# Decoder trunk mixer: where the output weights' low parts stand, and how the conv norm's row sums are formed

## Chip, cores, metric

The kernel runs on one core of a Trainium2 chip. The metric is device microseconds of one execution; the time before is the median of three runs, 1797.14 us (1795.66 to 1797.37). The engines are named as in the profile: PE (TensorE matrix products), PEld (its weight loads), DVE (VectorE), ACT (ScalarE), POOL (GpSimd), SP (SyncE, which issues most transfers). Each engine works through its own queue in order.

## The reference

Two layers, each with a gated feed-forward block, a mixer, and a second feed-forward block, over 512 tokens of width 1024, batch 1, all in float32. The change is in the mixer:

```python
h = rms_norm(x, mix_norm[l])
a, g, q, k, v = jnp.split(h @ w_in[l], splits, axis=-1)

conv_out = conv_module(a, g, conv_w[l], conv_b[l], conv_norm[l])
...
diff_out = diff_attention(q, k, v, rel_bias, lam, lam_init, subln_norm[l])
x = x + jnp.concatenate([conv_out, diff_out], axis=-1) @ w_out[l]

def conv_module(a, g, conv_w, conv_b, conv_norm):
    u = a * jax.nn.sigmoid(g)
    y = lax.conv_general_dilated(u, rhs, ...)   # causal, depthwise, 31 taps, 512 channels
    y = y + conv_b
    return jax.nn.silu(rms_norm(y, conv_norm))  # the norm runs over the 512 channels of a token

# differential attention: 4 heads, two softmax maps each (64 wide), values 128 wide
a = p[:, :, 0] - lam * p[:, :, 1]
o = einsum(a, v);  o = rms_norm(o, subln_g) * (1.0 - lam_init)
```

## The kernel before

**Tiling.** Activations lie with channels on the 128 partitions and the 512 tokens along the row, in 8 blocks of 128 channels. Weights arrive as float32 chunks of 128 x 1024. Each is split into a rounded high part (`whi`, ACT, line 97) and the rest, the low part (`wlo`, line 98, on DVE or POOL as the call says). A product of two float32 matrices is then three products in the faster rounded type (`mm3`: lines 160, 163, 164).

**Order.** The program is written as one stream and a scheduler that is part of the build (`TileContext` with its timeline) puts each engine's instructions into an order of its own choosing, which is then fixed; `keep_in_program_order` holds a single instruction back from being moved ahead of what was written before it. A tile in a pool with n buffers can be written again only when the reader of n tiles earlier is done. PSUM has eight banks, by tag: `sc` 2, `po` 2, `mm` 2, `tp` 1, `y` 1.

**The mixer** (`mixer`). First the projections: conv inputs (`conv_in`), keys and queries (`project`, `to_features`), values (`project_values`). Then two things run side by side.

- The conv branch. `conv_taps(c, n)` forms channel block c of 4. For c = 0 POOL adds all 31 taps (each product on ACT at line 662, each addition on POOL at line 663, into `yp`); for c = 1 and 2 DVE does all taps in a PSUM bank `y` (line 675); for c = 3 POOL does 10 taps and DVE 21, and line 679 joins the two into `u`. `conv_square` squares a block on ACT (line 649) and POOL adds the squares into `csum` (line 650). `conv_finish` then takes the token sums of `csum` over partitions: `rows_rstd` transposes four 128 x 128 blocks into PSUM (line 216), DVE sums each row (line 220) and scales it (line 221), POOL raises it to the power -1/2 (`rs_y`, line 209). `spread` puts the 512 factors on a diagonal (`diag`, DVE, line 236), multiplies by ones so that every partition has them (line 240, bank `y`), and ACT copies that to `rb` (line 244). Then for each of the four blocks: multiply by `rb` (POOL, line 689), tanh (ACT, line 691), the swish's product (DVE, line 692), the high part (ACT, line 693) and the low part (DVE, line 694), which are the right-hand operands of the first half of the output projection.
- Attention. 16 steps (i, h), query block i from 3 down to 0, head h. `softmaxes` makes two score products (line 709; map 0 in an `sc` bank, map 1 in a `po` bank), adds the bias and takes a minimum on DVE (line 713), exponentials and their sums on ACT (line 717), then the small factors on DVE (reciprocal, line 720; `c2`, line 722) and the combined map `e0` (line 723). Line 723 reads the `po` bank, so the score two steps later waits for it. Two steps later `keys_first` transposes the map (line 730) and ACT copies it (line 732); a step after that `values` multiplies by the values (line 739, bank `mm`). After the last head of a block come the block's norm (DVE 746 and 750, POOL 751 and 209, DVE 754 `ov`), and `block_out` transposes it (line 766) and writes its high and low part (ACT 768, DVE 769). The `mm` banks are two, so block 1's value products need block 3's outputs written.

**The output projection** follows (`chunk(wout[...], G)`, line 815): half 0 of the weights times the conv branch, half 1 times attention's outputs. Its low parts are made on POOL. Its first four chunks are loaded long before they are used, and the scheduler may put their low parts wherever POOL seems free. The results go to banks `sc` and `po`, and DVE adds them to x (line 820).

Of the kernel before, what the change touches and what calls it, by code (L numbers as in the profile page):

```python
# [11 lines left out]
F32 = mybir.dt.float32  # L12
# [3 lines left out]
ALU = mybir.AluOpType  # L16
AX = mybir.AxisListType

P = 128
# [4 lines left out]
NT = SEQ // P  # L24
# [3 lines left out]
CC = 512  # L28
CT = CC // P
# [7 lines left out]
EPS = 1e-6  # L37
# [30 lines left out]
def trunk(ctx: ExitStack, tc: tile.TileContext, xt, par, lamv, relb, onehot,  # L68
          gu1, dn1, wag, wqkv, wout, gu2, dn2, out):
    nc = tc.nc  # L70
    V, S, G, T = nc.vector, nc.scalar, nc.gpsimd, nc.tensor

    const = ctx.enter_context(tc.tile_pool(name="const", bufs=1))
    small = ctx.enter_context(tc.tile_pool(name="small", bufs=2))
# [6 lines left out]
    def f32(ap):  # L81
        return ap.bitcast(F32)
# [3 lines left out]
    def bank(tag, name):  # L86
        return psum.tile([P, 512], F32, tag=tag, name=name, bufs=BANKS[tag])
# [4 lines left out]
    def ring(tag, n=1024):  # L92
        dt = F32 if "raw" in tag else F32R
        return wp.tile([P, n], dt, tag=tag, name=tag, bufs=RING[tag])

    def parts_of(raw, hi, lo, eng=None):
        S.activation(hi, raw, AF.Copy)  # L97
        (eng or V).tensor_tensor(out=lo, in0=raw, in1=f32(hi), op=ALU.subtract)  # L98

    def chunk(src, eng=None):  # L100
        raw, hi, lo = ring("wraw"), ring("whi"), ring("wlo")
        nc.sync.dma_start(raw, src)
        parts_of(raw, hi, lo, eng)
        return hi, lo

    def gather(src, blocks, eng=None):
# [51 lines left out]
    def mm3(ps, w, x, start, stop, pin=False):  # L158
        (wh, wl), (xh, xl) = w, x
        first = T.matmul(ps, wh, xh, start=start, stop=False)  # L160
        if pin:
            tc.keep_in_program_order(first)
        T.matmul(ps, wh, xl, start=False, stop=False)  # L163
        T.matmul(ps, wl, xh, start=False, stop=stop)  # L164
# [21 lines left out]
    for k0, k1 in ((0, 1), (1, 4), (4, KT)):  # L186
        h = slice(k0 * P, k1 * P)
# [9 lines left out]
    ones = const.tile([P, P], F32, tag="ones", name="ones")  # L197
# [9 lines left out]
    def rsqrt(v, n, use=""):  # L207
        y = small.tile([P, n], F32, tag=f"rs_y{n}{use}", name="rs_y")
        G.tensor_tensor(y, v, mhalf[:, :n], op=ALU.pow)
        return y  # L210

    def rows_rstd(s, dim, use="", pin=False):

        ps = bank("y", "ps_rows")
        for j in range(NT):
            mm = T.transpose(ps[:, j * P : (j + 1) * P], s[:, j * P : (j + 1) * P], ident)
            if pin:
                tc.keep_in_program_order(mm)
        v = small.tile([P, NT], F32, tag=f"rowv{use}", name="rowv")
        V.tensor_reduce(v, ps.rearrange("p (j c) -> p j c", j=NT), axis=AX.X, op=ALU.add)  # L220
        V.tensor_scalar(v, v, 1.0 / dim, EPS, op0=ALU.mult, op1=ALU.add)
        return rsqrt(v, NT, use), v

    def spread(rc, tag, pin=False, split=False):

        parts, dt, left = [rc], F32, ones
        if split:
            hi = small.tile([P, NT], F32R, tag="rc_hi", name="rc_hi")
            V.tensor_scalar(hi, rc, 1.0, None, op0=ALU.mult)
            lo = small.tile([P, NT], F32, tag="rc_lo", name="rc_lo")  # L230
            V.tensor_tensor(lo, rc, f32(hi), op=ALU.subtract)
            parts, dt, left = [f32(hi), lo], F32R, ones_r
        ps = bank("y", "ps_spread")
        for n, part in enumerate(parts):
            dg = tmp.tile([P, NT, P], dt, tag=("diag", "sq")[n], name="diag", bufs=1 + n)
            V.tensor_tensor(
                dg, ident.unsqueeze(1).broadcast_to([P, NT, P]),
                part.unsqueeze(2).broadcast_to([P, NT, P]), op=ALU.mult,
            )
            mm = T.matmul(ps, left, dg.rearrange("p j c -> p (j c)"), start=n == 0, stop=n == len(parts) - 1)  # L240
            if pin:
                tc.keep_in_program_order(mm)
        r = act.tile([P, SEQ], F32, tag=tag, name=tag)
        S.activation(r, ps, AF.Copy)
        return r
# [254 lines left out]
    nlam, gq, gsub, ghalf = [], [], [], []  # L500
# [35 lines left out]
    def mixer(l, pr, after):  # L536
        with tc.tile_pool(name="mix", bufs=1) as mp, tc.tile_pool(name="mt", bufs=2) as mt:
# [102 lines left out]

            ys = [None] * CT
            csum = mp.tile([P, SEQ], F32, tag="csum", name="csum")

            def conv_square(c, y):
                if c == 0:
                    S.activation(csum, y, AF.Square)
                else:
                    sq = mt.tile([P, SEQ], F32, tag="csq", name="csq", bufs=1)
                    S.activation(sq, y, AF.Square)
                    G.tensor_tensor(csum, csum, sq, op=ALU.add)  # L650

            def conv_taps(c, n):

# [27 lines left out]
                    S.activation(ys[c], y, AF.Copy)  # L681
                conv_square(c, ys[c])

            def conv_finish():
                rcv = spread(rows_rstd(csum, CC, "c")[0], "rb")
                for c in range(CT):
                    z = ys[c]
                    hg = ghalf[l][:, c : c + 1]
                    G.tensor_tensor(z, z, rcv, op=ALU.mult)
                    th = mt.tile([P, SEQ], F32, tag="gl", name="th", bufs=1)  # L690
                    S.activation(th, z, AF.Tanh, scale=hg)
                    V.scalar_tensor_tensor(z, th, 1.0, z, op0=ALU.add, op1=ALU.mult)
                    S.activation(ch[:, c, :], z, AF.Copy, scale=hg)
                    V.scalar_tensor_tensor(cl[:, c, :], z, hg, f32(ch[:, c, :]), op0=ALU.mult, op1=ALU.subtract)
# [5 lines left out]
            def softmaxes(i, h):  # L700
                W = (i + 1) * P
                tq = slice(i * P, W)
                if h == 0:
                    sums[i] = small.tile([P, 2, HEADS], F32, tag="sums", name="sums")
                scs = [bank(tag, "ps_sc")[:, :W] for tag in ("sc", "po")]
                e0 = mt.tile([P, SEQ], F32, tag="e0", name="e", bufs=4)[:, :W]
                sm = sums[i]
                for m in range(2):
                    T.matmul(scs[m], qz[:, m, h, tq], kt[:, h, :W], start=True, stop=True)  # L709

                for m, (sc, e) in enumerate(zip(scs, (e0, scs[1]))):
                    mn = small.tile([P, 1], F32, tag=f"mn{m}", name="mn")
                    V.tensor_tensor_reduce(
                        out=e, in0=sc, in1=row["bias"][:, h, SEQ - W :], scale=1.0, scalar=3e38,
                        op0=ALU.add, op1=ALU.min, accum_out=mn,
                    )
                    S.activation(e, e, AF.Exp, bias=mn, scale=-1.0, accum_out=sm[:, m, h : h + 1])

                r2 = small.tile([P, 1], F32, tag="r2", name="r2")
                V.reciprocal(r2, sm[:, 1, h : h + 1])  # L720
                c2 = small.tile([P, 1], F32, tag="c2", name="c2")
                V.tensor_scalar(c2, r2, nlam[l], sm[:, 0, h : h + 1], op0=ALU.mult, op1=ALU.mult)
                V.scalar_tensor_tensor(e0, scs[1], c2, e0, op0=ALU.mult, op1=ALU.add)
                maps[i, h] = e0

# [47 lines left out]
            def attend(n):  # L773
                if n < len(steps):
                    softmaxes(*steps[n])
                if 2 <= n < len(steps) + 2:
                    keys_first(*steps[n - 2])
                if 3 <= n < len(steps) + 3:
                    values(*steps[n - 3])
                if n >= 5 and steps[n - 5][1] == HEADS - 1:  # L780
                    block_out(steps[n - 5][0])
# [19 lines left out]
                project_values(NT - 2 - 2 * n)  # L801
            for c in range(CT):
                conv_taps(c, POOL_TAPS[c])
            for n in range(2, len(steps) + 5):
                attend(n)
            conv_finish()

            for half, t in ((0, slice(0, SEQ)), (1, slice(SEQ // 2, SEQ)), (1, slice(0, SEQ // 2))):  # L810
                if t.stop == SEQ:
                    w = [None] * 4
                for m in range(KT):
                    if w[m // 2] is None:
                        w[m // 2] = chunk(wout[l, half, m // 2], G)
                    ps = bank(("sc", "po")[m % 2], "ps_out")[:, : t.stop - t.start]
                    for kk in range(4):
                        k = half * 4 + kk
                        mm3(ps, wpart(w[m // 2], (m % 2) * 4 + kk), (ch[:, k, t], cl[:, k, t]), kk == 0, kk == 3)
                    V.tensor_tensor(x[:, m, t], ps, x[:, m, t], op=ALU.add)  # L820

                    if half == 1 and t.start == 0 and m < KT // 2:
                        after(m)
# [103 lines left out]
```

## Time and profile before

| quantity | value |
|---|---|
| median of three runs | 1797.14 us |
| profiled execution, its own time | 1795.63 us |
| its span, first to last instruction | 1793.9 us |
| PE busy | 1783.0 us (99%) |
| DVE, ACT, POOL busy | 1207.6, 897.1, 666.8 us |
| granted TensorE clock | 1.000 over the span |

The span is what the trace covers; the execution's own time has 1.7 us more around it. PE is busy nearly all the time by the page, but a matmul's end is modelled, and matmuls overlap; whether TensorE is held up is read from the starts in its timeline and from its waits.

The main rows that the change touches, with their mean durations:

| row | what | count | mean ns |
|---|---|---|---|
| L98 POOL, 128x1024 | low part of a weight chunk | in the mixer | 2400 |
| L663 POOL | one conv tap's addition | 78 | 1295 |
| L650 POOL | squares into `csum` | 6 | 1292 |
| L216 PE, from `csum` | one transpose of the row sums | 8 | 273 |
| L220 DVE | the sums over rows (all uses) | 8 | 690 |
| L739 PE | one record of a value product (two each) | 160 | 278 |
| L722 DVE | the factor `c2` | 32 | 268 |
| L746 DVE | a small product of two SBUF operands | 8 | 158 |

The conv norm runs at 487 to 497 us in layer 0 and 890.8 us later in layer 1; the two layers agree to about 0.1 us in that stretch.

### The profile page before, as it was taken

Reading aid. Unit: us, or ns where it says so; the run is one execution under the profiler, and the core shown is the slowest. Engines: PE = TensorE matmul, PEld = TensorE weight load, DVE = VectorE, ACT = ScalarE, POOL = GpSimd, SP = SyncE. Lnnn points to the kernel's source line nnn. Section 1 sums busy time; section 2 is a strip of 40 time slices with the busy share of each in tenths; the row PEclk is TensorE's granted clock in tenths of the full one; section 3 lists DMA queues with packets and bytes.
Section 4 is the critical chain, followed back from the end, with each engine's and each line's share of the span. In section 5 each row is a group of like instructions: output and inputs, shape, how many; then the busy total and the mean of one; then the engine's idle time right before and its main releaser. Section 6 shows DMA issues by size and latency. Waiting matters only on the chain.

```text
span 1793.9 us, 28355 instructions
## 1 busy us (share of the span) xinstructions
PE 1783.0 (99%) x10845; PEld 1590.0 (89%) x10845; DVE 1207.6 (67%) x1862; ACT 897.1 (50%) x1482; POOL 666.8 (37%) x460
## 2 busy tenths in 40 slices
PE   9999999999999999999999999999999999999999
PEld 7899899888788899899888998998887888998997
DVE  6977476568867867477576764765788587663762
ACT  5555265445844456266433643644558354552651
POOL 4243242269843133133102312412797332422420
PEclk9999999999999999999999999999999999999999
DMA  7466476423212367366334664663231133664651
GB/s 243 109 171 188 108 185 173 123 89 94 71 48 83 94 165 189 105 171 191 104 94 98 171 167 123 178 175 118 71 116 50 48 106 93 166 177 112 180 150 59
DMA packets 111721, 231.24 MB, mean 129 GB/s; under 512 B 12151, under 2 KB 33414, under 8 KB 111584
## 3 DMA queue, kind: packets, MB, share of 16 engines
q1 hardware_dynamic: 91488, 191.93, 33.4%
q0 software_dynamic: 19808, 37.33, 12.8%
q8 instruction: 85, 1.39, 0.3%
q14 instruction: 52, 0.43, 0.1%
q10 hardware_dynamic: 288, 0.16, 0.0%
HBM read 227.26 MB, written 3.42 MB: 129 GB/s over the span
## 4 chain that ended last, share of the span: by engine, by line
PE 96%; DVE 2%; ACT 1%; issue 1%; DMA 0%; ACTq 0%; DVEq 0%
PE ps_pair L379 38%; PE ps_d L164 9%; PE ps_d L160 9%; PE ps_d L163 9%; PE ps_pair L163 5%; PE ps_pair L164 5%; PE ps_pair L160 5%; PE ps_pair L592 2%; PE ps_pair L593 2%; PE ps_pair L591 2%; PE ps_out L160 1%; PE ps_out L163 1%; PE ps_sc L709 1%; PE ps_out L164 1%; DVE actl L258 1%; PE ps_v L623 1%
## 5 line engine op out<-in xcount | busy, mean ns | idle before, releaser
L97 ACT ACTIVATE whi<-wraw 128x512 fp32r<-128x512 f32 (+2 forms) x600 | 467.2, 802 | 607.5 <-PE ps_pair L379 223.2
L98 DVE TENSOR_TENSOR wlo<-wraw,whi 128x512 fp32r<-128x512 f32 (+2 forms) x556 | 521.3, 960 | 212.5 <-ACT whi L97 207.3
L379 PE MATMUL ps_pair<-acth,wlo 128*128 128x256 f32 x1088 | 307.9, 283 | 0.0
L379 PE MATMUL ps_pair<-actl,whi 128*128 128x256 f32 x1088 | 307.9, 283 | 0.0
L379 PE MATMUL ps_pair<-acth,whi 128*128 128x256 f32 x1088 | 307.9, 283 | 0.0
L163 PE MATMUL ps_d<-hl,whi 128*128 128x512 f32 x704 | 273.9, 389 | 0.0
L164 PE MATMUL ps_d<-hh,wlo 128*128 128x512 f32 x704 | 273.0, 389 | 0.0
L160 PE MATMUL ps_d<-hh,whi 128*128 128x512 f32 x704 | 268.4, 389 | 0.0
L143 POOL TENSOR_TENSOR wraw<-wraw 128x512 f32<-128x512 f32 x68 | 112.8, 1658 | 344.6 <-DMA wraw<-in_gu 286.2
L379 PE MATMUL ps_pair<-th,wlo 128*128 128x256 f32 x816 | 230.9, 283 | 0.0
L379 PE MATMUL ps_pair<-tl,whi 128*128 128x256 f32 x816 | 230.8, 283 | 0.0
L379 PE MATMUL ps_pair<-th,whi 128*128 128x256 f32 x816 | 230.8, 283 | 0.0
L138 POOL DMA_DIRECT2D wraw<-in_gu x68 | 82.0, 1205 | 374.9 <-DMA wraw<-in_gu 258.5
L379 PEld LDWEIGHTS ps_pair<-acth,whi 128*128 128x128 f32 x1088 | 208.9, 192 | 0.3
L379 PEld LDWEIGHTS ps_pair<-actl,whi 128*128 128x128 f32 x1088 | 208.9, 192 | 0.3
L379 PEld LDWEIGHTS ps_pair<-acth,wlo 128*128 128x128 f32 x1088 | 208.9, 192 | 0.0
L475 DVE SCALAR_TENSOR_TENSOR x<-ps_d,x 128x512 f32<-128x512 f32 x96 | 64.7, 688 | 180.5 <-PE ps_d L164 180.1
L160 PE MATMUL ps_pair<-acth,whi 128*128 128x512 f32 x448 | 173.8, 392 | 1.4 <-ACT whi L97 1.4
L163 PE MATMUL ps_pair<-actl,whi 128*128 128x512 f32 x448 | 174.7, 391 | 0.3 <-DVE actl L258 0.2
L164 PE MATMUL ps_pair<-acth,wlo 128*128 128x512 f32 x448 | 173.9, 390 | 0.0
L379 PEld LDWEIGHTS ps_pair<-tl,whi 128*128 128x128 f32 x816 | 156.5, 192 | 0.7
L379 PEld LDWEIGHTS ps_pair<-th,whi 128*128 128x128 f32 x816 | 156.5, 192 | 0.6
(174 smaller groups left out, 3268.8 us busy)
## 6 DMA issues: line engine op xcount, KB each, us to landing
wraw<-in_gu SPq DMA_DIRECT2D x208, 256.0 KB, 4.1
wraw<-in_gu SPq DMA_DIRECT2D x104, 512.0 KB, 3.7
wraw<-in_gu POOLq DMA_DIRECT2D x68, 512.0 KB, 5.8
wraw<-in_wqkv SPq DMA_DIRECT2D x24, 512.0 KB, 3.6
wraw<-in_dn SPq DMA_DIRECT2D x84, 128.0 KB, 3.1
wraw<-in_dn SPq DMA_DIRECT2D x32, 256.0 KB, 3.0
wraw<-in_wag SPq DMA_DIRECT2D x16, 512.0 KB, 3.6
wraw<-in_wout SPq DMA_DIRECT2D x16, 512.0 KB, 3.7
```

Source lines behind the costliest of these rows:

```text
L97: S.activation(hi, raw, AF.Copy)
L98: (eng or V).tensor_tensor(out=lo, in0=raw, in1=f32(hi), op=ALU.subtract)
L138: nc.gpsimd.dma_start(two.rearrange("p (b c) -> p b c", b=2), u[:, h[0]].unsqueeze(1).broadcast_to([P, 2, 512]), accum_op=ALU.add)
L143: G.tensor_tensor(more[:, h[0]], two[:, h[1]], whole[:, h[0]], op=ALU.add)
L160: first = T.matmul(ps, wh, xh, start=start, stop=False)
L163: T.matmul(ps, wh, xl, start=False, stop=False)
L164: T.matmul(ps, wl, xh, start=False, stop=stop)
L379: mm = T.matmul(ps, l, r, start=first and i == j == 0, stop=False, skip_group_check=True)
L475: V.scalar_tensor_tensor(x[:, m, :], ps, 0.5, x[:, m, :], op0=ALU.mult, op1=ALU.add)
L591: T.matmul(ps[n], xh[:, t], wh, start=k == 0, stop=False)
L592: T.matmul(ps[n], xh[:, t], wl, start=False, stop=False)
L593: T.matmul(ps[n], xl[:, t], wh, start=False, stop=k == KT - 1)
```

## The change

Four edits in `mixer` and its helpers.

- `chunk` and `parts_of` take `pin`; a pinned low part keeps its place in the written order. The four chunks of half 0 of the output weights are now asked for explicitly with `pin=True`: two right after the conv taps and the norm's rows, two behind `conv_finish`.
- The last channel block's squares are not added into `csum`; they stay in a tile of their own. `conv_rows` replaces `rows_rstd` here: for each 128 tokens, two products with one column of ones, the squares as the stationary operand, one from `csum` and one from the last block, summed in PSUM. Four numbers per partition result, which one DVE instruction scales before `rsqrt`.
- `conv_rows` is written straight after the taps, and `conv_finish` inside the attention loop behind step 9 instead of behind the loop.
- `c2` is formed by `scalar_tensor_tensor` with the sums as a tensor operand, where `tensor_scalar` had them as a second scalar.

```diff
-    def parts_of(raw, hi, lo, eng=None):
+    def parts_of(raw, hi, lo, eng=None, pin=False):
         S.activation(hi, raw, AF.Copy)
-        (eng or V).tensor_tensor(out=lo, in0=raw, in1=f32(hi), op=ALU.subtract)
-
-    def chunk(src, eng=None):
+        low = (eng or V).tensor_tensor(out=lo, in0=raw, in1=f32(hi), op=ALU.subtract)
+        if pin:
+            tc.keep_in_program_order(low)
+
+    def chunk(src, eng=None, pin=False):
         raw, hi, lo = ring("wraw"), ring("whi"), ring("wlo")
         nc.sync.dma_start(raw, src)
-        parts_of(raw, hi, lo, eng)
+        parts_of(raw, hi, lo, eng, pin)
         return hi, lo
...
             csum = mp.tile([P, SEQ], F32, tag="csum", name="csum")
+            csq = []
...
                     S.activation(sq, y, AF.Square)
-                    G.tensor_tensor(csum, csum, sq, op=ALU.add)
+                    if c == CT - 1:
+                        csq.append(sq)
+                    else:
+                        G.tensor_tensor(csum, csum, sq, op=ALU.add)
...
-            def conv_finish():
-                rcv = spread(rows_rstd(csum, CC, "c")[0], "rb")
+            def conv_rows():
+
+                v = bank("y", "ps_crow")[:, :NT]
+                for j in range(NT):
+                    for n, s in enumerate((csum, csq[0])):
+                        T.matmul(v[:, j : j + 1], s[:, j * P : (j + 1) * P], ones[:, :1], start=n == 0, stop=n == 1)
+                vs = small.tile([P, NT], F32, tag="rowvc", name="rowv")
+                V.tensor_scalar(vs, v, 1.0 / CC, EPS, op0=ALU.mult, op1=ALU.add)
+                return rsqrt(vs, NT, "c")
+
+            def conv_finish(rcv):
+                rcv = spread(rcv, "rb")
...
-                V.tensor_scalar(c2, r2, nlam[l], sm[:, 0, h : h + 1], op0=ALU.mult, op1=ALU.mult)
+                V.scalar_tensor_tensor(c2, r2, nlam[l], sm[:, 0, h : h + 1], op0=ALU.mult, op1=ALU.mult)
...
             for c in range(CT):
                 conv_taps(c, POOL_TAPS[c])
+
+            rcv = conv_rows()
+            wo = [chunk(wout[l, 0, n], G, pin=True) for n in range(2)]
             for n in range(2, len(steps) + 5):
                 attend(n)
-            conv_finish()
+                if n == 9:
+                    conv_finish(rcv)
+                    wo += [chunk(wout[l, 0, n], G, pin=True) for n in range(2, 4)]
...
             for half, t in ((0, slice(0, SEQ)), (1, slice(SEQ // 2, SEQ)), (1, slice(0, SEQ // 2))):
                 if t.stop == SEQ:
-                    w = [None] * 4
+                    w = [None] * 4 if half else wo
```

## The prediction

> **What bounds the kernel now.** I read the chain of waits first. It belongs almost wholly to TensorE, so a change counts only where it makes TensorE wait or gives it other work.
>
> ```profile
> PE 96%; DVE 2%; ACT 1%; issue 1%; DMA 0%; ACTq 0%; DVEq 0%
> ```
>
> TensorE's own waits (line waited at, who ended it: total, times, longest) say where the other 4% is. The mixer is the only stage with more than a startup wait, once in each layer:
>
> ```profile
> PE ps_out L160 <- ACT acth L693: 2.5, 2, 1.3
> PE ps_at L730 <- ACT at L732: 0.9, 2, 0.4
> PE ps_o L739 <- ACT at L732: 0.4, 2, 0.2
> ```
>
> The windows over layer 0's attention (columns: window, length, then busy time and count of PE, PEld, DVE, ACT, POOL) show who is short there. From 490 to 510 us VectorE has no free time, and TensorE loses most of its time there:
>
> ```profile
> 470.00:480.00 10.00, 10.00 (x48) 6.83 (x47) 6.53 (x20) 9.81 (x20) 10.00 (x6) 1.00 0.47 133
> 490.00:500.00 10.00, 9.53 (x64) 7.61 (x62) 9.80 (x35) 7.66 (x26) 4.67 (x5) 1.00 0.00 0
> 500.00:510.00 10.00, 8.66 (x47) 6.63 (x48) 10.00 (x36) 8.75 (x25) 3.99 (x5) 1.00 0.01 2
> ```
>
> TensorE's timeline shows the place: the first output product waits for the first channel block of the conv branch.
>
> ```profile
> 499.43 0.38 PE L730 MATMUL ps_at<-ident,e 128*128 128x128 f32 x2
> 501.08 0.49 PE L160 MATMUL ps_out<-acth,whi 128*128 128x512 f32 x1 [1.26 <-ACT acth L693]
> ```
>
> The POOL timeline shows why that block is late: low parts of the output weights (L98, 2.4 us each) stand between the last conv taps, and then comes the norm.
>
> ```profile
> 469.30 2.42 POOL L98 TENSOR_TENSOR wlo<-wraw,whi 128x1024 fp32r<-128x1024 f32 x1
> 471.68 1.28 POOL L663 TENSOR_TENSOR yp<-yp,prod 128x512 f32<-128x512 f32 x1
> 472.91 4.71 POOL L98 TENSOR_TENSOR wlo<-wraw,whi 128x1024 fp32r<-128x1024 f32 x2
> ...
> 483.92 1.27 POOL L663 TENSOR_TENSOR yp<-yp,prod 128x512 f32<-128x512 f32 x1 [0.16 <-ACT prod L662]
> 487.40 1.27 POOL L650 TENSOR_TENSOR csum<-csum,csq 128x512 f32<-128x512 f32 x1 [2.21 <-ACT csq L649]
> ...
> 491.51 1.01 POOL L209 TENSOR_TENSOR rs_y<-rowv,mhalf 128x4 f32<-128x4 f32 x1 [1.58 <-DVE rowv L221]
> 496.35 1.28 POOL L689 TENSOR_TENSOR yp<-yp,rb 128x512 f32<-128x512 f32 x1 [3.82 <-ACT rb L244]
> 497.58 3.64 POOL L689 TENSOR_TENSOR u<-u,rb 128x512 f32<-128x512 f32 x3
> ```
>
> And two like VectorE rows, of which the first ran beside POOL's multiplications (497.58 to 501.22) and the second did not:
>
> ```profile
> 498.97 1.30 DVE L692 SCALAR_TENSOR_TENSOR yp<-th,yp 128x512 f32<-128x512 f32 x1
> 501.92 0.68 DVE L692 SCALAR_TENSOR_TENSOR u<-th,u 128x512 f32<-128x512 f32 x1
> ```
>
> So a VectorE instruction with two tensors in SBUF waits until POOL's running instruction ends: 0.62 us here, and POOL's next one then took 1.54 us instead of 1.2, since it waited for VectorE. [...]
>
> **The change, part by part.** All times are on the clock of layer 0 before; layer 1 is the same 890.8 us later.
>
> What is removed: four transposes (4 x 0.109 = 0.44 us of TensorE), VectorE's row sum L220 (0.69) and POOL's last csum addition (1.29). Added are eight one-column products. The page has none. An fp32 product leaves two records (L739: 160 records for 80 products), so 16 records. The lower bound is 0; L739's distance of 0.112 us from start to start with 128 columns gives 1.8; its weight load's mean of 0.191 gives 3.1. I take 1.8, as nearest. The c2 step goes from L722 (0.27) to the form of L746 (0.16): some 0.1 us of VectorE for each of 16.
>
> Moved first: POOL's last six tap additions are no longer interrupted, so they follow ACT's products. ACT does two of these earlier, 2 x 0.61 us ahead of the exponentials; the last product ends at about 476.3, the last addition at 477.7 instead of 485.2. The combined channel block u follows at 478.5, its square on ACT at 480.4. The ACT delay reaches the map of step (3,2), written 0.9 us later (478.5 for 477.58), but has gone by the next score, whose bias is added at 480.75 (480.92 before). The one-column products stand behind the transposes and value products of (3,2); TensorE gets there at 482.0 and is through at 483.5. The row value follows map (2,0) on VectorE, at 483.7, and rs_y (1.02 on POOL) ends at 484.8, against 492.5 before: 7.7 us earlier. That is what the change wins.
>
> What stands next on each queue decides. In the changed program's order POOL goes from rs_y straight to two pinned low parts (2 x 2.4), then the four multiplications by rb (4.9), two more low parts (4.8), and only then the query blocks' sums and rs_y for blocks 3 and 2 (1.2 each). On VectorE diag stands next for the spread, and it reads two SBUF tensors. The rows of before have 0.12 us from rs_y to diag with POOL idle; now the low part starts at once and diag comes behind it: 2.4 + 0.6, done at 487.85 instead of 485.5. Queued behind diag are the bias of (2,3), map (2,1) and all later maps; behind the spread on TensorE all later scores. TensorE reaches the spread at about 486.6 and waits 1.3 us, which also covers the one-column products: without that cover they cost 1.8 - 0.44 = 1.4 us a layer.
>
> From there VectorE's queue, with the durations of its rows (bias 0.47, 0.34 or 0.2 by width, map 0.55 or 0.43, recip and c2 0.2, L692 0.6, L694 0.66): map (2,1) to 489.15, (2,2) to 491.3 after its exponential, the block 3 reduce to 492.4, map (2,3) to 494.0. Now L692 for yp waits for POOL's third multiplication (to 495.15, 1.15 us), L694 for a low part (to 498.15, 1.2 us), the second L692 for the other one (to 501.2, 1.95 us). Sum of these waits with diag's: 2.3 + 1.15 + 1.2 + 1.95 = 6.6 us, the last two behind POOL instructions of 2.4 us. Then bias, map (1,1), L694 and L692 (504.3), biases, block 2's reduce (505.5), ov of block 3 (506.3), L694, map (1,2), L692 (508.0), ov of block 2 (508.6, rs_y at 506.8), and the low part of block 3's outputs, L769, at 509.25. The value products of block 1 need block 3's bank free, so they wait for that L769, and in the new order they stand just ahead of the first output product: 509.4 + 4 x 0.22 = 510.3.
>
> Now the comparison. From the first 128x512 score at 472.05 to the first output product both orders hold the same attention products on TensorE: 4, 8, 8 and 5 scores of 512, 384, 256 and 128 columns, 34 map transposes, 32 value products, the spread; the new one has four more block transposes (0.44) for the four row transposes. Before, output products (0.227 each) filled TensorE from 501.08 on while VectorE finished; now none stands in front of that point. Shift: 510.3 - 501.1 = 9.2 us, less the 0.44 us done already, less what TensorE lost before behind 501.08: by the starts in its timeline to 511.6, 1.6 us over the usual distances (0.25 at 501.96, 0.28 at 506.74, 0.20 at 507.52, and smaller). Behind 510.3 I count no wait: over 40 us of output products cover the last maps. That is 7.2 us a layer, 14.4 in two. The span of 1793.9 becomes 1808.3, that execution's 1795.63 becomes 1810.0, and the median of the runs, 1.5 us above it, 1811.5.
>
> **Rivals.** [...]
>
> More waits: c2 now reads two SBUF tensors as well, so five of its sixteen, beside POOL's work from 484.8 to 501, would wait too. Laid out the same way the first output product comes at 512.2: 9.1 us a layer, 1815.3. The rows with small operands do not tell: the se step beside a low part (477.46) took 0.19 us, for 0.15 with POOL idle, with at most 0.15 us of the low part left. [...]
>
> The other side, faster: the conv branch, 6 us earlier at L689 (490.2 for 496.35), removes the wait of 1.26 us at the first output product, and attention keeps pace. The price if every loss of this stretch goes: 4.7 us a layer over the usual distances (3.1 up to 501.08 and 1.6 behind), less 1.4 for the one-column products: 3.3 a layer, 1790.5. It decides if the first output product stands before 503.1 (501.1 + 1.6 + 0.44). For it: the wait is on the page, and the norm does end earlier. Against it: VectorE is full from 490 on, and the change takes only 0.69 us and small c2 savings from it.
>
> No change: the waits moved are as long as those gone; 1797.
>
> **How the numbers follow.** Forecast 0.55; c2 waits too 0.12; order alone 0.15; faster 0.11; no change 0.07. A measurement of this kernel can tell 0.2%, 3.6 us, from no change. The order alone (+4.4) lies close to that, so 0.04 of it goes to no difference: faster 0.11, same 0.11, slower 0.78. Low end 1798, which leaves out the faster case and most of no change; high end 1818, above the c2 case with the products at their upper bound uncovered (2 x 1.3). The likeliest one's own range is 1805 to 1818.
>
> **What would show it.** In the changed kernel: POOL's tap additions end near 477.7 and rs_y near 484.8; diag takes about 2.9 us beside a low part, and L692 and L694 show 1.5 to 2.5 us; TensorE waits about 1.3 us at the spread; the first output product starts near 510. It is wrong if diag takes 0.7 us, or if the first output product starts before 503.

## The result, and the profile after

The changed kernel takes 1816.45 us (median of four runs, 1813.98 to 1818.35), the kernel before 1796.40 (four runs beside it, 1795.56 to 1797.37): a ratio of 1.011 with a 95% interval of 1.0098 to 1.0123. It is slower. The profiled execution took 1813.98 us, the quickest of the four, with a span of 1812.2, which is 18.3 more than before.

The chain of waits of the changed kernel has more of VectorE in it:

```profile
PE 95%; DVE 3%; issue 1%; ACT 0%; DMA 0%; DVEq 0%; ACTq 0%
```

TensorE's own waits (line waited at, who ended it: total, times, longest) were 2.5 us for the conv branch before. Now it waits for VectorE, and at four places that the list of before did not have:

```profile
PE ps_sc L725 <- DVE mn L729: 4.8, 8, 0.9
PE ps_sc L725 <- DVE e L739: 3.8, 5, 1.5
PE ps_spread L242 <- DVE diag L238: 2.3, 2, 1.1
PE ps_o L782 <- DVE ov L770: 2.1, 3, 0.9
```

Windows of layer 0 (length, then busy time and count of PE, PEld, DVE, ACT, POOL; then the granted clock):

```profile
480.00:490.00 10.00, 8.86 (x57) 6.91 (x56) 8.48 (x16) 5.19 (x14) 6.02 (x3) 1.00 0.15 47
490.00:500.00 10.00, 7.43 (x44) 5.14 (x43) 9.51 (x25) 5.46 (x16) 9.92 (x9) 1.00 0.33 111
500.00:510.00 10.00, 6.92 (x32) 5.03 (x33) 9.92 (x33) 9.23 (x26) 1.98 (x3) 0.86 0.17 54
508.00:511.00 3.00, 2.96 (x15) 2.27 (x14) 3.00 (x11) 1.59 (x3) 0.00 (x0) 0.57 0.02 5
```

From 490 to 500 us VectorE is as busy as before (9.51 for 9.80), but with 25 instructions where it had 35. TensorE falls from 9.53 to 7.43. And for 3.4 us from 507.15 on the granted clock is 0.50, which it was nowhere in this stretch before.

POOL's timeline, to set beside that of before:

```profile
475.08 2.63 POOL L669 TENSOR_TENSOR yp<-yp,prod 128x512 f32<-128x512 f32 x2 [0.86 <-ACT prod L668]
483.98 1.02 POOL L211 TENSOR_TENSOR rs_y<-rowv,mhalf 128x4 f32<-128x4 f32 x1 [6.26 <-DVE rowv L697]
484.96 5.12 POOL L98 TENSOR_TENSOR wlo<-wraw,whi 128x1024 fp32r<-128x1024 f32 x2
490.03 1.27 POOL L705 TENSOR_TENSOR yp<-yp,rb 128x512 f32<-128x512 f32 x1
...
494.41 4.67 POOL L98 TENSOR_TENSOR wlo<-wraw,whi 128x1024 fp32r<-128x1024 f32 x2
499.02 0.66 POOL L767 TENSOR_TENSOR so<-so,se 128x4 f32<-128x4 f32 x1
```

And VectorE's timeline, the four instructions that took far longer than usual, all beside those low parts:

```profile
485.03 2.83 DVE L238 TENSOR_TENSOR diag<-ident,rs_y 128x512 f32<-128x512 f32 x1
...
488.45 1.64 DVE L738 SCALAR_TENSOR_TENSOR c<-r,nlam,sums 128x1 f32<-128x1 f32 x1
...
494.60 2.18 DVE L738 SCALAR_TENSOR_TENSOR c<-r,nlam,sums 128x1 f32<-128x1 f32 x1
...
497.58 2.05 DVE L708 SCALAR_TENSOR_TENSOR yp<-th,yp 128x512 f32<-128x512 f32 x1
```

In kernel e8 below, which makes no low parts here, these take 0.69 us (diag), 0.22 (c2, but for two beside POOL's multiplications) and 0.68 (L708). The first c2 ends at 490.09, with the low part (490.08). So the four lost 2.14, 1.42, 1.96 and 1.37 us: 6.9 a layer. TensorE's timeline shows what comes of it:

```profile
488.01 1.10 PE L242 MATMUL ps_spread<-diag,ones 128*128 128x512 f32 x2 [1.15 <-DVE diag L238]
...
507.24 1.12 PE L782 MATMUL ps_o<-ident,ov 128*128 128x128 f32 x4 [0.91 <-DVE ov L770]
...
511.33 0.47 PE L162 MATMUL ps_out<-acth,whi 128*128 128x512 f32 x1
```

The first output product starts at 511.33, before at 501.08. The four block transposes at 507.24 take 1.12 us; at the full clock, before, four took 0.60 to 0.66.

### The profile page after: what moved, and what is told of

Its sections match the earlier page's. It is cut to its first block, busy times and chain, and to the rows that moved or that the text cites. A ratio compares the mean times of both kernels' runs of the same rounds, so it can differ in the third digit from the quotient of the medians.

```text
span 1812.2 us, 28396 instructions
## 1 busy us (share of the span) xinstructions
PE 1791.5 (99%) x10869; PEld 1595.4 (88%) x10869; DVE 1223.4 (68%) x1860; ACT 897.6 (50%) x1482; POOL 660.8 (36%) x458
## 4 chain that ended last, share of the span: by engine, by line
PE 95%; DVE 3%; issue 1%; ACT 0%; DMA 0%; DVEq 0%; ACTq 0%
PE ps_pair L381 38%; PE ps_d L166 9%; PE ps_d L162 9%; PE ps_d L165 9%; PE ps_pair L165 5%; PE ps_pair L166 5%; PE ps_pair L162 5%; PE ps_pair L594 2%; PE ps_pair L595 2%; PE ps_pair L593 2%; PE ps_out L162 1%; PE ps_out L166 1%; PE ps_out L165 1%; PE ps_sc L725 1%; PE ps_v L625 1%; PE ps_v L623 1%
## 5 line engine op out<-in xcount | busy, mean ns | idle before, releaser
L145 POOL TENSOR_TENSOR wraw<-wraw 128x512 f32<-128x512 f32 x68 | 107.1, 1574 | 349.1 <-DMA wraw<-in_gu 281.2
```

Of the source, the lines that this page charges most:

```text
L145: G.tensor_tensor(more[:, h[0]], two[:, h[1]], whole[:, h[0]], op=ALU.add)
```

## Experiments

All kernels are compared on one table. "Stretch" is the time from the first 128x512 score to the last output product of a layer, taken from TensorE's starts; it leaves out what happens elsewhere in the run. "VectorE over" adds up, for the VectorE instructions that start 15 to 60 us after a layer's first 128x512 score, what each took beyond the duration that the quickest fifth of its kind (line, operation and shape) stays within. "Clock lost" is one minus the granted clock, summed over windows of 2.5 us across 45 us of each layer. The last three are from one profiled execution each. The medians of the kernel before were 1796.0 to 1796.4 beside all of these.

| kernel | median us | ratio, 95% | stretch, layers 0 and 1 | VectorE over | clock lost |
|---|---|---|---|---|---|
| before | 1796.4 | | 94.6, 94.6 | 2.0, 2.1 | 0, 0 |
| after | 1816.5 | 1.0098 to 1.0123 | 102.8, 103.5 | 8.1, 8.1 | 1.7, 1.7 |
| e1 after, old c2 | 1813.8 | 1.0083 to 1.0116 | 103.9, 102.4 | 6.1, 6.2 | 5.1, 3.4 |
| e2 low parts late | 1817.0 | 1.0102 to 1.0132 | 105.4, 105.2 | 7.2, 7.1 | 5.1, 5.1 |
| e3 before, new c2 | 1797.7 | 0.9998 to 1.0016 | 95.6, 94.6 | 5.5, 3.5 | 0, 0 |
| e4 before, new row sums | 1799.1 | 1.0009 to 1.0028 | 96.2, 96.2 | 2.7, 2.7 | 0, 1.7 |
| e5 after, not pinned | 1800.6 | 1.0018 to 1.0038 | 97.3, 96.5 | 5.2, 3.4 | 0, 0 |
| e6 before, pinned | 1799.8 | 1.0009 to 1.0028 | 96.1, 96.2 | 5.1, 5.1 | 0, 0 |
| e7 low parts in four | 1814.1 | 1.0085 to 1.0119 | 103.3, 102.3 | 6.0, 6.0 | 3.4, 3.4 |
| e8 after, no low parts | 1804.7 | 1.0033 to 1.0063 | 97.7, 99.3 | 2.2, 2.2 | 0, 1.7 |
| e9 four low parts first | 1807.3 | 1.0045 to 1.0075 | 100.7, 99.5 | 7.9, 7.9 | 1.7, 0 |
| e10 before, no low parts | 1798.2 | 1.0001 to 1.0020 | 94.6, 94.6 | 1.8, 1.8 | 0, 0 |
| e11 e8, old row sums | 1797.2 | 0.9994 to 1.0013 | 94.7, 94.8 | 2.5, 2.6 | 0, 0 |
| e12 e8, old c2 | 1805.1 | 1.0032 to 1.0062 | 100.7, 99.4 | 1.6, 1.6 | 3.4, 1.7 |

Five theories were set against each other. P: low parts on POOL hold VectorE's instructions while they run, as the prediction had it. Q: they only make POOL's own queue late. O: the new order of TensorE's products costs. Then, for what was left, R: a low part costs where VectorE has no idle time, and the residue comes from the one-column products and c2. S: the early norm itself costs. Every edit also lets the scheduler choose other orders for VectorE and TensorE, so a pair of kernels seldom differs by its edit alone.

### The parts alone: c2 and the row sums

```diff
# e1 (in after) and, the other way round, e3 (in before)
-                V.scalar_tensor_tensor(c2, r2, nlam[l], sm[:, 0, h : h + 1], op0=ALU.mult, op1=ALU.mult)
+                V.tensor_scalar(c2, r2, nlam[l], sm[:, 0, h : h + 1], op0=ALU.mult, op1=ALU.mult)
# e4: before, with conv_rows of after, at the old place
-                rcv = spread(rows_rstd(csum, CC, "c")[0], "rb")
+                rcv = spread(conv_rows(), "rb")
```

> The changed kernel with c2 formed by tensor_scalar again, all else as changed. [...] If c2 were the whole cause: 1803 or less.

> The kernel before with the new c2 alone. Theory P: c2 waits for the tap additions and low parts that run on POOL up to 485 us, 0.3 to 1.2 us each for six of them, where VectorE still has free time; 1796 to 1801. [...]

> The kernel before with the one-column products in place of the transposes and the sum, nothing pinned, conv_finish at its old place. Both theories: TensorE has 1.4 us a layer more, VectorE 0.7 and POOL 1.3 less, and the norm ends some 2 us earlier; 1794 to 1799. If the products themselves cost what was lost: above 1805.

With the old c2 the waits at c2 are gone, but VectorE's next instructions meet the low parts instead. VectorE's timeline of e1:

```profile
488.58 0.27 DVE L738 TENSOR_SCALAR c<-r,nlam,sums 128x1 f32<-128x1 f32 x1
...
496.44 1.50 DVE L710 SCALAR_TENSOR_TENSOR actl<-yp,ghalf,acth 128x512 fp32r<-128x512 f32 x1
...
498.26 2.44 DVE L708 SCALAR_TENSOR_TENSOR u<-th,u 128x512 f32<-128x512 f32 x1
```

c2 takes 0.27 us beside a low part where it took 1.64. The sum of VectorE's loss falls from 8.1 to 6.1 in layer 0, while the clock lost rises. The median is 2.7 us lower, in P's range of 1810 to 1815 and below O's 1815 to 1818, but the intervals of the two kernels overlap, so this gain isn't told from none. In the kernel before (e3) the new c2 makes no difference in time that can be told, as P had it, though it is held there too, at a place where VectorE has idle time in the kernel before. VectorE's timeline of e3, beside a low part that POOL makes from 481.35 to 483.73:

```profile
482.20 1.55 DVE L722 SCALAR_TENSOR_TENSOR c<-r,nlam,sums 128x1 f32<-128x1 f32 x1
```

The row sums alone (e4) cost 3.1 us in two layers (1799.1; 1794 to 1799 was expected), near the 2.7 that the products take: 16 records, 0.112 us from start to start, 1.8 a layer, less the four transposes' 0.44.

### The low parts: later, not pinned, shorter, gone, earlier

```diff
# e2: the four low parts are written behind step 13 instead
+                if n == 13:
+                    for raw, hi, lo in lows:
+                        tc.keep_in_program_order(G.tensor_tensor(out=lo, in0=raw, in1=f32(hi), op=ALU.subtract))
# e5: after, the four chunks with pin=False
# e6: before, with this behind the taps
+            wo = [chunk(wout[l, 0, n], G, pin=True) for n in range(4)]
# e7: after, a pinned low part in four instructions of 256 columns
+        for c in [slice(j, j + 256) for j in range(0, 1024, 256)] if pin else [slice(None)]:
+            low = (eng or V).tensor_tensor(out=lo[:, c], in0=raw[:, c], in1=f32(hi)[:, c], op=ALU.subtract)
# e8: after; a pinned chunk makes no low part
+        return (hi, hi) if pin else (hi, lo)
# e9: after; all four chunks ahead of the row sums
+            wo = [chunk(wout[l, 0, n], G, pin=True) for n in range(4)]
             rcv = conv_rows()
```

> The changed kernel with the four low parts of the output weights written behind attention step 13, so that on POOL they stand behind the four multiplications by rb and the sums of blocks 3 and 2; rows, c2 and the place of conv_finish stay as changed. Theory P: diag takes 0.7 us instead of 2.8, only waits of about 0.5 us behind POOL's 1.2 us multiplications stay; what is left is the order: 2 to 4 us a layer over before, 1800 to 1805. Theory O: the output products stand no earlier in TensorE's queue, so 1813 to 1818.

> The changed kernel with its four low parts not pinned; everything else of the change stays. The built order puts the low parts back between the last conv taps on POOL. [...] Theory O (the loss is in the new order of TensorE's products, not in the low parts): 1811 to 1818.

> The kernel before with one edit: its four low parts asked for and pinned right behind the conv taps. The row sums, the place of conv_finish and c2 are those of before. POOL then makes four low parts in a row at about 479 to 490 us, ahead of the row value. P: VectorE's instructions with two operands in SBUF take 1.5 to 3 us beside them, and the norm comes later: 1804 to 1818. Q: POOL's queue is late by up to 9.6 us less what the low parts between the taps took before, 1800 to 1812. O: 1795 to 1800.

> The changed kernel with each pinned low part made by four instructions of 256 columns in the same place, so that POOL has the same work and VectorE finds it free every 0.6 us. P: diag about 1.2 us at most, c2 at most 0.9, so that of the 7.1 us of waits a layer at diag, c2 and the swish product 4 to 6 go: 1804 to 1811. Q: POOL's queue is as late as before or by the fixed part of twelve more instructions later: 1814 to 1820. O: 1813 to 1819.

> The changed kernel without the four low parts of half 0 (the low part's product is made with the high part in its place, so TensorE has the same number of products). On POOL everything else keeps its order. P and Q: the multiplications by rb follow at once, the first output product comes at 500 to 503 us or before, and the time is 1788 to 1800. O: the new order stays as slow, 1811 to 1818.

> The changed kernel with all four pinned low parts right behind the conv taps, ahead of the row value; the rest of the change stays. POOL then makes them at 477.7 to 487.5 us in layer 0, where VectorE still has idle time, and none in the stretch from 490 on, where it has none. Theory R (a low part costs what VectorE waits for it in its full stretch, 6 us a layer in the changed kernel, and what TensorE, starved by that, loses by the lower clock): 1800 to 1805, with a clock of 1.00 throughout, though the row value comes 3 us later on POOL. Theory S (it is the early norm and the order around it that cost, wherever the low parts are made): 1806 to 1816.

**Gone (e8), not pinned (e5).** Without the low parts 11.7 us of the 20 disappear (1816.45 to 1804.74), 5.9 a layer, on the same order of everything else on POOL; VectorE's and TensorE's built orders differ. That is close to what VectorE loses less in layer 0 (8.1 less 2.2). Put back between the taps (e5), the time is 1800.6, as P and Q had it (1796 to 1802), though the rest of the change is still there. So O is wrong as the whole cause. But 8.7 us stay without a low part; P and Q, which had 1788 to 1800, missed that.

**Later (e2).** P expected 1800 to 1805, and it came out at 1817, inside O's 1813 to 1818. The waits at diag and L708 did go, and came back at the new place. POOL's, then VectorE's timeline of e2:

```profile
503.22 9.71 POOL L833 TENSOR_TENSOR wlo<-wraw,whi 128x1024 fp32r<-128x1024 f32 x4
```

```profile
505.50 2.91 DVE L713 SCALAR_TENSOR_TENSOR actl<-u,ghalf,acth 128x512 fp32r<-128x512 f32 x1
...
508.79 1.84 DVE L741 SCALAR_TENSOR_TENSOR c<-r,nlam,sums 128x1 f32<-128x1 f32 x1
```

TensorE starves beside them (1.08 us busy of 5.00), and works at a clock of 0.50 for ten microseconds (5.1 us of clock lost). TensorE's timeline, then the windows of e2:

```profile
508.92 0.79 PE L728 MATMUL ps_sc<-kt,qz 128*128 128x128 f32 x2 [4.23 <-DVE e L742]
```

```profile
505.00:510.00 5.00, 1.08 (x4) 0.82 (x4) 5.00 (x5) 0.41 (x1) 5.00 (x3) 0.66 0.50 139
510.00:515.00 5.00, 3.94 (x14) 3.41 (x14) 4.14 (x18) 2.30 (x10) 2.93 (x2) 0.50 0.70 199
```

This is also the cleanest pair for the price of a low part. In layer 0, e2 and e8 have the same order on TensorE and VectorE past the first output product, and counted from the first score their instructions start within 0.2 us of each other up to the low parts. Then e2 has four low parts, the first output product comes 55.4 us after the first score instead of 49.7, and the time is 12.3 us longer (1816.99 for 1804.74), 6.1 a layer. The 4.23 us are a wait for a map on VectorE, which stands there behind the held `actl`, not for anything that POOL makes: that is P's mechanism, and neither Q's nor O's, though the time fell in O's range.

**Shorter (e7).** What diag loses falls from 2.1 to 0.5, the longest wait to 0.8, and VectorE's loss over that of before from 6.1 to 4.0 in layer 0. P expected that 4 to 6 us of it would go, and 1804 to 1811; about 2 went, and it was 1814.1, where Q and O were. POOL's second pair now takes 7.81 us where it took 4.67 (whether its pieces wait for VectorE in turn is not shown), and the sum for query block 3 starts at 502.90 instead of 499.02. POOL's timeline and the windows of e7:

```profile
495.13 7.81 POOL L99 TENSOR_TENSOR wlo<-wraw,whi 128x256 fp32r<-128x256 f32 x8
502.90 0.19 POOL L767 TENSOR_TENSOR so<-so,se 128x4 f32<-128x4 f32 x1
```

```profile
500.00:505.00 5.00, 2.65 (x12) 1.96 (x12) 5.00 (x15) 4.64 (x15) 4.32 (x7) 0.88 0.43 136
505.00:510.00 5.00, 4.41 (x12) 3.17 (x11) 3.83 (x15) 1.45 (x5) 1.22 (x1) 0.50 0.16 64
```

What VectorE loses beside the low parts went down by about 2 us a layer, and POOL's lateness and 3.4 us more of lost clock took most of it back. The two can't be told apart here.

**Earlier (e6, e9).** In e6 the low parts run from 481.4 to 490.7, still beside VectorE, which is held there. VectorE's timeline of e6:

```profile
484.36 1.72 DVE L223 TENSOR_SCALAR rowv<-rowv 128x4 f32<-128x4 f32 x1
...
486.83 1.56 DVE L748 SCALAR_TENSOR_TENSOR se<-sums 128x4 f32<-128x4 f32 x1
```

P had 1804 to 1818 for that and Q 1800 to 1812; it was 1799.8, inside O's 1795 to 1800. Before 490 VectorE has idle time (it was 80% busy from 480 to 490 in the kernel before), and a wait that falls into it can cost little. In e9, the changed kernel with the same move, c2 waits twice, and longer than in the changed kernel. POOL's, then VectorE's timeline of e9:

```profile
479.15 9.30 POOL L98 TENSOR_TENSOR wlo<-wraw,whi 128x1024 fp32r<-128x1024 f32 x4
```

```profile
479.12 2.40 DVE L738 SCALAR_TENSOR_TENSOR c<-r,nlam,sums 128x1 f32<-128x1 f32 x1
...
483.95 2.20 DVE L738 SCALAR_TENSOR_TENSOR c<-r,nlam,sums 128x1 f32<-128x1 f32 x1
```

VectorE loses 7.9 us a layer in e9, nearly as much as in the changed kernel (8.1), yet e9 is 9.1 us faster (1807.3). So it isn't the length of the waits that sets their price, but where they fall. Measured from e8, four low parts cost 1.3 us a layer at 479 to 488, and 5.9 where the change puts them; the orders of VectorE and TensorE that go with each place are part of both figures. R had 1800 to 1805 and a clock of 1.00, and S 1806 to 1816: the time is in S's range, and one layer lost 1.7 us of clock. R's figure left out the residue of e8, the next question.

### The residue without low parts

```diff
# e10: before; a chunk of half 0 makes no low part
+        return (hi, hi) if none else (hi, lo)
# e11: e8, conv_rows as before, and the third addition into csum
+                return rows_rstd(csum, CC, "c")[0]
# e12: e8, c2 as before
+                V.tensor_scalar(c2, r2, nlam[l], sm[:, 0, h : h + 1], op0=ALU.mult, op1=ALU.mult)
```

> The kernel before without the four low parts of half 0 (the product is made with the high part in its place). POOL's last taps are then not interrupted, and the norm comes some 7 us earlier than before, with the row sums and c2 of before. Theory S (an early norm costs by itself, because its VectorE work then stands ahead of attention's): 1800 to 1805, near the 1804.7 of the changed kernel without low parts. Theory R (the residue of 8.7 us there comes from the one-column products and c2): 1790 to 1798.

> The changed kernel without the four low parts (high part in their place) and with the row sums of before (a third addition into csum, four transposes, VectorE's sum). If the one-column products make the residue: 1799 to 1802, 3 to 5 us under the 1804.7 with them. If not: 1803 to 1807.

> The changed kernel without the four low parts (high part in their place) and with c2 by tensor_scalar as before. If c2's waits beside POOL's multiplications (0.43 and 0.37 us in layer 0 of the run without low parts) lie on the path: 1802 to 1804, up to 2 us under 1804.7. If something else ends those steps: 1804 to 1806.

With the old row sums (e11) the residue is gone: 1797.2, 7.5 us less than e8. That is 3.75 a layer, where the products' own time, less the transposes, is 1.4; both expected ranges (1799 to 1802, and 1803 to 1807) lie above it. Windows from 20 to 35 us after each kernel's first score, first e8, then e11:

```profile
477.63:492.63 15.00, 15.00 (x98) 12.12 (x96) 12.51 (x42) 11.69 (x34) 5.30 (x6) 1.00 0.02 6
```

```profile
479.18:494.18 15.00, 15.00 (x99) 12.23 (x97) 13.68 (x48) 12.31 (x36) 5.31 (x7) 1.00 0.02 5
```

TensorE is full in both. In e8 it spends part of that on one-column products, and VectorE works 1.2 us less. But 0.7 of that is no loss: it is e11's row sum (0.68 and 0.15 us), for which e8 has one instruction of 0.16. What is left, some 0.5 us, agrees with a gap in VectorE's timeline of e8, where it waits for the score behind the one-column products:

```profile
484.60 0.57 DVE L729 CUSTOM_DVE_ANT_0 ps_sc<-ps_sc,bias 128x384 f32<-128x384 f32 x1 [0.59 <-PE ps_sc L725]
```

The stretches differ by 3.0 us in layer 0 and 4.5 in layer 1, where one lower-clock period (up to 1.7) comes on top. The products' own 1.4 and this 0.5 don't make up the 3.0. The built orders differ too: e8 has the transposes of query block 2 ahead of its first output product, which starts 49.7 us after the first score, and e11 has them behind it, at 45.2. What share the order has was not taken apart, and e4, the same exchange in the kernel before, cost 1.5 a layer. So the price of the products lies between 1.5 and 3.75 a layer, and why it is more than 1.4 here is not shown.

Old c2 in e8 (e12) gave nothing: 1805.1, in a scatter of 1801.95 to 1807.5; without a gain 1804 to 1806 was expected. Taking all low parts out of the kernel before (e10) gave nothing either. Its profiled execution reached the first score 7 us late, after waits near 130 us that have nothing to do with the mixer, but the stretch is 94.6, as before, though `rs_y` starts 27.4 us after the first score instead of 34.0. The time lies just above R's 1790 to 1798 and below S's 1800 to 1805. Between the two this speaks for R's cause, but no gain came: in this kernel an earlier norm wins nothing. Its first output product stands 45.5 us after the first score, in an order of its own, for 43.6 before; what an earlier norm would be worth in the old order is not shown.

So the 20 us split, each step by its own pair and with the change of order that goes with it: low parts 11.7 (after to e8), the way of the row sums 7.5 (e8 to e11), early norm, place of `conv_finish` and c2 together about 1 (e11 to before). Starting from the kernel before, single edits cost 3.7 (pin), 3.1 (row sums) and 1.7 (c2, not told from zero): 8.5 together. The other 11.5 were not taken apart: e6 pins the low parts at another place than the change does, and the earlier place of `conv_finish` was never run alone. No variant that computes everything was faster than the kernel before.

## Why the prediction was right, and where it was off

The direction, the mechanism and the place held; the time is 5 us above the forecast and inside the likeliest one's own range. Of the 5 us, 4.0 are in the profiled execution (1813.98 for 1810.0); the median lies 2.5 us above it, not 1.5. The other three executions have a mean granted clock of 0.996 where this one has 0.998, by estimate 3.6 us of 1815. By its steps:

- **The reading at the start**: TensorE's waits can't be where the chain's other 4% is. All of them add up to 6.4 us, 0.4% of the span. Nothing in the sum hangs on this.
- **POOL up to the row value**: taps end at 477.71 (forecast 477.7), `rs_y` at 485.0 (484.8). Right.
- **diag behind a low part**: 2.83 us (2.9), TensorE waits 1.15 at the spread (1.3). Right.
- **The waits that follow**: forecast L692, L694 and L692 again for 1.15, 1.2 and 1.95 us. Only the first came (1.4), and behind a low part, not behind POOL's third multiplication; the other two places were taken by c2, at 1.4 and 2.0. The sum of four was forecast as 6.6 and is 6.9; with two of its terms at other instructions, that it came so close is partly luck. So c2 did wait, as the rival had it, but instead of the others rather than on top of them. That a 128x1 operand is held like a wide one was this rival's open point, and the trace settles it. e1 puts 1.3 us a layer on its waits, not told from none; the rival had 1.9.
- **The first output product**: forecast 510.3, measured 511.33. The step left out the granted clock: the block transposes at 507.24 start about 0.21 us apart instead of 0.11, and the clock is back at 1.00 only at 510.57.
- **"Behind 510.3 I count no wait"**: TensorE's stretch grew by 8.2 and 8.9 us in the two layers. More is lost behind it: the next stage's first products wait for `actl` (L260), 0.9 us in total, for 0.2 before.
- **One-column products at nothing, "covered" by the wait at the spread**: the 1.8 us they take is right, the price is the weakest step. Where that wait is absent, the prediction had 1.4 a layer; e4 gives 1.5, and e8 against e11 3.75, part of which may be the order. In the changed kernel with its low parts the row sums alone were not undone, so whether nothing was right there stays open.
- **What the change wins**: a norm 7.7 us earlier. It came nearly as forecast (485.0 for 492.5), and still the first output product stands at 511.33, where the faster rival needed it before 503.1. In e10, without any low part beside it, an earlier norm brought nothing either.
- **The order alone**, +4.4 us in the chances, is the new order with no wait of VectorE beside POOL. No run shows this term: diag took 2.83 us beside a low part, and without any low part (e8) the kernel lay 8.7 us over the one before, part of it from the row sums.

The term that was mis-sized is the shift per layer, 7.2 forecast and 9.15 in the span. Of the 2 us between them 1.0 (layer 0) and 1.7 (layer 1) lie in the stretch, where the clock fell, and some 0.6 a layer outside it.

## To carry to other kernels

Price a moved instruction by whom it holds and whether that engine is short at the new place: the same four low parts held VectorE about as long in both places (7.9 us a layer in e9, 8.1 in the changed kernel), but cost 1.3 us a layer where it had idle time ahead, and 5.9 where it had none. The one-column products took 1.4 us more of TensorE a layer and cost 1.5 in one kernel and 3.75 in another; that they cost more where VectorE, behind TensorE, is short is the author's estimate and was not shown. And taking one wait beside POOL away pays little if the next instruction is held in its place: in e1 c2 went from 1.64 to 0.27 us, and then `actl` took 1.50 and L708 2.44; the 2.7 us that the time fell aren't told from none.

## What the runs showed of the hardware

- **Small operands were held too.** `c2`, with 128x1 operands, took up to 2.40 us (e9) beside POOL's subtractions of 2.4 (1.64 and 2.18 in the changed kernel), for 0.22 without, while its `tensor_scalar` form took 0.27 beside one (e1). A `tensor_scalar` on 128x4 (L223 in e6) took 1.72 there, for 0.15 in e11. Why one `tensor_scalar` is held and the other not, no run shows.
- **The clock fell with no wait of TensorE over 0.95 us in the 3.4 us ahead.** Windows of the changed kernel around the drop, then one of e8 that ends at a drop in layer 1:

```profile
503.50:506.90 3.40, 1.63 (x8) 1.15 (x8) 3.40 (x14) 3.40 (x10) 0.36 (x2) 1.00 0.00 0
507.00:507.50 0.50, 0.26 (x1) 0.27 (x2) 0.50 (x2) 0.50 (x4) 0.50 (x1) 0.65 0.00 0
```

```profile
1397.61:1401.02 3.41, 2.14 (x12) 1.49 (x12) 3.09 (x10) 2.00 (x7) 0.39 (x1) 1.00 0.00 0
```

  TensorE was busy 48% of the 3.4 us ahead, its longest wait there was 0.95 us, and then the clock was halved. In e8 it was halved at 1401.02, behind 3.41 us in which TensorE was 63% busy and waited no longer than 0.6 us at a time. The lost clock comes in steps, 0, 1.7, 3.4 or 5.1 us a layer in every row of the table; one step is 3.4 us at 0.50, as from 507.15 to 510.57 in the changed kernel. 63% busy didn't keep the clock up there. What makes it fall the runs don't show, nor that the busy share sets it: e8 had 3.4 us at 57% (502.0 to 505.4) and lost no clock in that layer, and e1 had 2.5 us at 6% (0.15 us busy, 1400.0 to 1402.5) at a clock of 1.00, with 0.96 in the 2.5 us behind it.
- **The lost clock takes part in what a gain is worth.** e1 and e7 took about 2 us a layer from VectorE's waits and lost three and two more such periods over both layers than the changed kernel, which has two; the kernel before has none.
